# Engine order of first operations on fetched data, and a new order of value products, in a hybrid attention layer

## The chip, the core and the metric

The kernel runs on one core of a Trainium2 chip. The core has a matrix engine (TensorE, PE in the profile), three engines for elementwise work (VectorE or DVE, ScalarE or ACT, GpSimd or POOL), and a queue engine (SyncE or SP) that issues transfers. Each engine works through its own list of instructions strictly in order, and waits on semaphores for the others. Sixteen DMA engines carry the transfers of all queues. The metric is the device time of one execution in microseconds; lower is better.

## The reference

One decoder layer with two groups of heads, over 512 tokens of width 2048, in float32:

```
h = rms_norm(x, g_pre);  proj = h @ w_in
q_lat, kv_lat, k_rope, gate_mla, fq, fk, fv, f_logit, gate_fox = split(proj)
o_mla = softmax_causal(MLA scores of q_lat, kv_lat, k_rope) @ v  * silu(gate_mla)
c = cumsum(log_sigmoid(f_logit + b_forget))
o_fox = softmax_causal(fq·fk * scale + c_q - c_k) @ fv           * silu(gate_fox)
out = x + rms_norm(concat(o_mla, o_fox) @ w_out, g_post)
```

There are 8 MLA heads and 8 FoX heads of width 128. The change touches the first third of the work: the first projection, the gates, queries, keys and values of the FoX heads, and the FoX scores.

## The kernel before

**Arithmetic.** A float32 operand is kept as two parts, hi (rounded to the matrix engine's format by an ACT copy) and lo (the rest, by a DVE subtraction); a product is three matrix passes, hi·hi, hi·lo and lo·hi (mm3, L142 to L144). So each weight chunk that is fetched (tile raw) goes through one ACT cast (whi, L269) and one DVE subtraction (wlo, L272) before PE can use it. Casts and subtractions run two chunks ahead of PE, loads four chunks ahead (chunk).

**Products.** Some columns of the input projection (the FoX values, called v, and others) are computed by Winograd's variant of Strassen's scheme: seven products p1, p2, p4, q6, g3, g5, g7 of half-size blocks, of x blocks or sums of them, with weight blocks or sums of them. The sums of x blocks are made on DVE, written to memory by POOL (away_steps) and fetched back (fetch) into slots, where part_fetched splits them into hi and lo. Sums of weight blocks are of two kinds. Some are joined on chip: a chunk brings a second tile, and join adds it (L259). The others are made in memory by **background steps**: add_step copies one block (on SP's queue, L305) and a POOL transfer adds the other to it (L302). A small write called mark (L307), from a weight tile that is cast just then, paces them. set_pace(n) says that one step is made every n tiles; paced counts one tile per k step in projections and products, whether it belongs to the steps' own work or not. The first projection isn't counted. There are 36 steps, and state["pace"] is 6 at the start. load asserts that a step is far enough on when its sum is loaded.

**Order of the first third.** proj_first (L576), a projection for the forget logits and part of the latents, in 16 k steps; its engines' order is fixed by hand (manual_schedule). Then fox_g(0) (gate projection), product p1, fox_g(1), p2, fox_g(2), g5, fox_q(0), g3, p4, q6, fox_k(0), g7. A gate, q or k projection has 16 k steps, a product 8. scaled and scaled_copy combine the products' results into the blocks c11, c12, c21, c22 of the values; v_out writes them to memory, load_v fetches them by pairs of heads, split_v splits them. Then four rounds of two FoX heads follow: queries, scores, keys, values, each pumped as small steps from the list todo between the matmuls of the next projection. enqueue_scores and enqueue_values fill that list; drain runs what is left of it.

**Who sets an engine's order.** Outside the hand-ordered part a scheduler takes, at compile time, any instruction whose inputs it models as ready, so that one may go ahead of earlier ones of its engine's program. keep_in_program_order takes an instruction out of that: it stays behind those that come ahead of it in the program on its engine. Before the change only the join's addition (L259) and, in a late stage, the weight cast are pinned so.

**Other work on fetched data.** rotary_tables fetches the positions (pos, L803) and makes sine and cosine in 20 steps on DVE and ACT, the first being the cast of L811. forget_keys negates a fetched row c per head (nk, L789) and adds the mask.

**Memory.** Most tiles of 4 KB per partition come from 28 common slots (slot). The values' blocks and the table's tiles come from a pool of their own (vr, v_room), which is closed after g7, so that the heads' tiles (pp) take its place.

Of the kernel before, what the change touches and what calls it, by code (L numbers as in the profile page):

```python
# [65 lines left out]
def tile_hybrid_layer(  # L66
# [61 lines left out]
            act.mul(to, src[:, :P], scale)  # L128
        return to

    def split_into(hi, lo, src, scale=None):
        if scale is None:
            act.copy(hi, src)
            dve.tensor_tensor(out=lo, in0=src, in1=hi.bitcast(F32), op=ALU.subtract)
        else:
            act.mul(hi, src, scale)
            dve.scalar_tensor_tensor(  # L137
                out=lo, in0=src, scalar=scale, in1=hi.bitcast(F32), op0=ALU.mult, op1=ALU.subtract
            )
# [132 lines left out]
        dve.tensor_tensor(out=lo[:, :m], in0=raw[:, :m], in1=hi[:, :m].bitcast(F32), op=ALU.subtract)  # L272
        ready[i] = [t[:, :m].rearrange("p (k c) -> p k c", k=n) for t in (hi, lo)]

    state = {"loaded": 0, "divided": 0, "tiles": 0, "step": -1, "pace": 6}

    def prepare(i):
        while state["divided"] < min(len(chunks), i + 1):
# [80 lines left out]

    first = add_chunks(w_in, [(0, O_KR - L4, KL), (KL, O_F, NH)], NK, 2, KL + NH, single=2)  # L360
    fox = [{} for _ in range(4)]
    for n in ("g0", "p1", "g1", "p2", "g2", "s5", "q0", "s3", "p4", "s6", "k0", "s7",
              "q1", "k1", "q2", "k2", "q3", "k3", "g3"):
        name = {"p1": "p1", "p2": "p2", "p4": "p4", "s5": "g5", "s3": "g3", "s6": "q6", "s7": "g7"}.get(n)
        if name:
            add_products([(name, "v")], plain_in)
        else:
            at = {"q": O_FQ, "k": O_FK, "g": O_GF}[n[0]] + 256 * (3 - int(n[1]))
            fox[int(n[1])][n[0]] = add_chunks(w_in, [(0, at, 256)], NK, 4, 256)
# [416 lines left out]
    def forget_keys(both, h):  # L786

        nk, nkm = both[:, 0, :], both[:, 1, :]
        dve.tensor_scalar(out=nk, in0=nk, scalar1=-1.0, scalar2=None, op0=ALU.mult)  # L789
        for b in range(NT):  # L790
            c = slice(b * P, (b + 1) * P)
            dve.tensor_tensor(out=nkm[:, c], in0=nk[:, c], in1=mask, op=ALU.add)
        return nk, nkm, h
# [5 lines left out]
    def rotary_tables():  # L799
# [7 lines left out]
        def names():  # L807
            nonlocal n1, n2
            nn = vr.tile([P, 2, S], F32, tag="c", name="nn")
            n1, n2 = nn[:, 0, :], nn[:, 1, :]  # L810
            dve.tensor_copy(n1, pi)  # L811
            dve.tensor_scalar(out=r, in0=n1, scalar1=ifc[:, 0:1], scalar2=None, op0=ALU.mult)

        n1 = n2 = None
# [148 lines left out]

    def part_fetched(n, of, j):
        both = oper[n, of][j]
        split_into(both[:, 0], both[:, 1], both[:, 1].bitcast(F32))

    def divisions(n, of):
        return [lambda j=j: part_fetched(n, of, j) for j in range(2 if of == "o" else 4)]
# [106 lines left out]
            ] + [pp.tile([P, 256], F32, tag="v3", name=f"{name}3", bufs=2)]  # L1076
        return v_tiles[name]

    def values_into(tiles, cols, parts, scale=lambda t: None):
        for t in range(NT - 1):  # L1080
            hi, lo = tiles[t]
            split_into(hi[:, cols], lo[:, cols], parts[t], scale(t))
        if scale(NT - 1) is None:
            act.copy(tiles[NT - 1][:, cols], parts[NT - 1])
        else:
            act.mul(tiles[NT - 1][:, cols], parts[NT - 1], scale(NT - 1))

    def values_of(name):
        tiles = v_tiles.pop(name)
# [40 lines left out]
    def split_v(pair, both):  # L1130

        tiles = v_pair(f"fv{pair}")
        return lambda: values_into(tiles, slice(0, 256), [both[:, t, :] for t in range(NT)])

    gates, gate_slots = {}, {}

# [12 lines left out]
    def v_block(name):  # L1149
        return vr.tile([P, 2, S], F32, tag="c", name=name)  # L1150
# [7 lines left out]
    def two_of(make, name):  # L1158
        return [make(f"{name}{i}") for i in range(2)]
# [18 lines left out]
    todo.extend(fs[:13])  # L1178
    fox_g(0, [att_bank("fg00"), bank("pv", "fg01", 1)])
    drain()  # L1180
    rot = rotary_tables()
    rot.append(rotary_key)
    wait(1)
# [16 lines left out]
    todo.extend([*x_steps(2), *x_steps(3)])  # L1200
    fox_g(2, two_of(proj_bank, "fg2"))
    drain()
    set_pace(16)
    f3, f6, f7 = (fetches(n, "m") for n in ("g3", "q6", "g7"))
    d3, d6, d7 = (divisions(n, "m") for n in ("g3", "q6", "g7"))
    G = two_of(att_bank, "vg")
# [1 line left out]
    c22 = v_block("vc22")  # L1208
    scaled(c22, G, 2, pb, ALU.subtract, rcol)
    todo.extend([*f3, *rot[10:14], *d3, *rot[14:]])  # L1210
    q, wholes = fox_q(0)
    drain()
    todo.extend([*f6[:2], lambda: None, lambda: None, d6[0], f6[2], d6[1], f6[3]])
    product("g3", "v", operand("g3", "m"), G, False, True)
    drain()
    c12 = v_block("vc12")
    scaled(c12, G, 0, pa, ALU.subtract, rcol)
    wait(1)
    todo.append(d6[2])
    wait(2)  # L1220
    todo.append(d6[3])
    B = two_of(proj_bank, "vp4")
    product("p4", "v", x_block(1, 2), B, True, True)
    c21 = v_block("vc21")
    scaled(c21, B, 2, pb, col=rcol)
    drain()
    set_pace(10)
    C = two_of(proj_bank, "vc")
    product("q6", "v", operand("q6", "m"), C, True, True)
    scaled(c12, C, 0, c12, col=rcol)  # L1230
    v_out(c12, 0, 1)
# [538 lines left out]
```

## Time and profile before

| what | us |
|---|---|
| three runs, median | 936.87 |
| lowest and highest | 936.67, 938.46 |
| the profiled execution, own time | 936.87 |
| its span in the profile | 935.1 |
| PE at work | 895.9 |

A row of the timeline gives start, length, engine, source line, operation, output tile and input tiles, and in brackets how long the engine stood idle just before and what ended that. A row of the busy times by stage gives the window, its length, then for each engine the microseconds at work and the number of instructions, then the clock granted to PE (1.00 is full), the mean share of the 16 DMA engines in use, and GB/s. A row of the waits gives who waited for whom, the sum, the number of times, and the longest. PE's matmuls overlap, so starts, not lengths, show its rate.

### The profile page before, as it was taken

The page shows a single profiled execution, that of the slowest core. Times are in us where ns is not written, and L with a number is a line of the kernel's source. Part 1 is how long each engine was busy: PE and PEld are TensorE (multiplying, and loading weights), DVE is VectorE, ACT ScalarE, POOL GpSimd, SP SyncE. Part 2 cuts the span into 40 slices and gives each one's busy share as a digit, 9 for nine tenths or more (in the row PEclk, how much of TensorE's full clock was granted, in tenths as well). Part 3 has the DMA queues.
Part 4 walks back from the last instruction along what each step waited for, and adds up shares of the span by engine and source line. Part 5 has one row for each costly group of instructions (what it writes and reads, how often), then busy time and mean ns, then how long its engine had stood idle before and what let it go on. Part 6 is the DMA issues. An engine that isn't in the chain of part 4 may idle for free.

```text
span 935.1 us, 12821 instructions
## 1 busy us (share of the span) xinstructions
PE 895.9 (96%) x4594; PEld 761.3 (81%) x4594; DVE 679.5 (73%) x1120; ACT 453.6 (49%) x836; POOL 65.8 (7%) x86
## 2 busy tenths in 40 slices
PE   4999996999999999999999999999999999999997
PEld 4988884777887887888999899878888888888885
DVE  1979783486368573766759879877779896897875
ACT  3684331344334341433455545654556566655474
POOL 1000220001021100100000000000000000000021
PEclk8899998899999999999999999999999999999998
DMA  9468999668899988889689998578843234789878
GB/s 296 119 198 234 287 303 342 195 221 265 220 281 256 248 206 226 237 207 266 147 310 399 345 332 291 136 176 202 217 110 107 68 113 159 247 313 304 282 221 251
DMA packets 125515, 218.26 MB, mean 233 GB/s; under 512 B 16362, under 2 KB 53764, under 8 KB 124428
## 3 DMA queue, kind: packets, MB, share of 16 engines
q1 hardware_dynamic: 113340, 179.41, 59.2%
q0 software_dynamic: 11376, 37.75, 19.5%
q8 instruction: 36, 0.59, 0.3%
q10 hardware_dynamic: 736, 0.29, 0.1%
q14 instruction: 27, 0.22, 0.1%
HBM read 202.72 MB, written 65.03 MB: 286 GB/s over the span
## 4 chain that ended last, share of the span: by engine, by line
PE 80%; DMA 10%; DVE 5%; ACT 3%; issue 1%; SPq 1%; POOL 0%; ACTq 0%; DVEq 0%
PE fk L142 3%; PE fk L143 3%; PE fk L144 3%; PE fg L142 3%; PE fg L143 3%; PE fg L144 3%; PE in L576 3%; PE fq L142 2%; PE fq L143 2%; PE fq L144 2%; PE sm L619 2%; DVE wlo L272 2%; DMA second<-in_w_in_dram 2%; DMA raw<-in_w_in_dram 2%; PE oa L144 2%; PE oa L143 2%
## 5 line engine op out<-in xcount | busy, mean ns | idle before, releaser
L272 DVE TENSOR_TENSOR wlo<-raw,whi 128x1024 fp32r<-128x1024 f32 (+3 forms) x217 | 256.2, 1187 | 118.7 <-ACT whi L269 109.7
L269 ACT CAST whi<-raw 128x1024 fp32r<-128x1024 f32 (+3 forms) x217 | 220.8, 1023 | 240.5 <-PE fg L143 28.0
L142 PE MATMUL fk<-h,whi 128*128 128x512 f32 x128 | 53.9, 421 | 0.0
L143 PE MATMUL fk<-h,whi 128*128 128x512 f32 x128 | 51.2, 400 | 0.0
L144 PE MATMUL fk<-h,wlo 128*128 128x512 f32 x128 | 51.2, 400 | 0.0
L142 PE MATMUL fq<-h,whi 128*128 128x512 f32 x128 | 50.8, 397 | 0.0
L142 PE MATMUL fg<-h,whi 128*128 128x512 f32 x128 | 50.3, 393 | 0.0
L144 PE MATMUL fq<-h,wlo 128*128 128x512 f32 x128 | 50.0, 390 | 0.0
L143 PE MATMUL fq<-h,whi 128*128 128x512 f32 x128 | 49.9, 390 | 0.0
L144 PE MATMUL fg<-h,wlo 128*128 128x512 f32 x128 | 49.9, 390 | 0.0
L143 PE MATMUL fg<-h,whi 128*128 128x512 f32 x128 | 49.9, 389 | 0.0
L259 DVE TENSOR_TENSOR raw<-raw,second 128x1024 f32<-128x1024 f32 x32 | 39.0, 1218 | 10.7 <-DMA second<-in_w_in_dram 10.6
L576 PE MATMUL in<-whi,h 128*128 128x328 f32 x128 | 30.8, 329 | 12.5 <-DVE h L137 12.5
L641 ACT ACTIVATE pf<-sf,stf 128x128 f32<-128x128 f32 (+3 forms) x32 | 16.8, 525 | 33.9 <-DVE stf L634 33.9
L576 PEld LDWEIGHTS in<-whi,h 128*128 128x128 f32 x128 | 22.1, 195 | 12.7 <-DVE h L137 12.7
L144 PEld LDWEIGHTS fk<-h,wlo 128*128 128x128 f32 x128 | 24.8, 193 | 5.7
L142 PE MATMUL mq<-ln,whi 128*128 128x512 f32 x72 | 29.0, 402 | 0.0
L142 PEld LDWEIGHTS fk<-h,whi 128*128 128x128 f32 x128 | 24.7, 193 | 4.7 <-issue 0.2
L143 PEld LDWEIGHTS fk<-h,whi 128*128 128x128 f32 x128 | 25.0, 195 | 4.1
L144 PEld LDWEIGHTS fq<-h,wlo 128*128 128x128 f32 x128 | 24.0, 188 | 5.3
L144 PEld LDWEIGHTS fg<-h,wlo 128*128 128x128 f32 x128 | 24.0, 188 | 5.2
L143 PE MATMUL mq<-ln,whi 128*128 128x512 f32 x72 | 28.2, 392 | 0.0
(556 smaller groups left out, 2481.0 us busy)
## 6 DMA issues: line engine op xcount, KB each, us to landing
raw<-in_w_in_dram SPq DMA_DIRECT2D x96, 512.0 KB
raw<-in_w_out_dram SPq DMA_DIRECT2D x32, 512.0 KB
second<-in_w_in_dram SPq DMA_DIRECT2D x24, 512.0 KB
bmg<-awaymg SPq DMA_DIRECT2D x20, 256.0 KB
awaymg<-rmg POOLq DMA_DIRECT2D x8, 512.0 KB, 10.8
raw<-t6v SPq DMA_DIRECT2D x8, 512.0 KB
t7o<-in_w_out_dram SPq DMA_DIRECT2D x4, 1024.0 KB
t7o<-in_w_out_dram POOLq DMA_DIRECT2D x4, 1024.0 KB, 10.3
```

The lines of the kernel that those rows point to most:

```text
L142: pe.matmul(o, ah, bh, start=first, stop=False, **kw)
L143: pe.matmul(o, ah, bl, start=False, stop=False, **kw)
L144: pe.matmul(o, al, bh, start=False, stop=last, **kw)
L259: tc.keep_in_program_order(dve.tensor_tensor(out=raw, in0=raw, in1=second, op=ALU.add))
L269: cast = act.copy(hi[:, :m], raw[:, :m])
L272: dve.tensor_tensor(out=lo[:, :m], in0=raw[:, :m], in1=hi[:, :m].bitcast(F32), op=ALU.subtract)
L576: pe.matmul(banks[t][:, :n], a[k][:, tss[t]], b[:, j, :], start=k == 0 and m == 0, stop=k == NK - 1 and m == 2,)
L619: pe.matmul(s[:, :nn], a[:, qs], c[:, :nn], start=(i == 0), stop=(i == len(pairs) - 1))
L641: act.activation(p, s[:, :n], AF.Exp, bias=st[:, 0:1], scale=unit, accum_out=st[:, 1:2])
```

## The change

- in_order(...) pins instructions with keep_in_program_order. Pinned are: both halves of the split of a fetched operand (part_fetched), the split of fetched values (split_v, and the last plain copy in values_into), the negation in forget_keys (L789), and the cast of the positions (L811).
- fox_k(0) moves from between q6 and g7 to between g3 and q6, and p4 from ahead of q6 to behind it; the weights' list is ordered to match (k0 and p4 change places). The fetches and splits of q6's operand go from g3 and p4 into fox_k(0), those of g7's operand from fox_k(0) into p4 and g7.
- The pace is 4 up to the end of fox_g(0), then 20 up to g5's end, 8 from fox_q(0) to fox_k(0), 12 from q6 to g7 (before: 6 up to fox_g(2)'s end, 16 from g5 to p4, 10 from q6 to g7).
- The last sums c22 and c21 go to common slots (vo22, vo21) rather than over their first operand in the values' pool.

```diff
+    def in_order(*instructions):
+        for i in instructions:
+            tc.keep_in_program_order(i)
...
-    def split_into(hi, lo, src, scale=None):
+    def split_into(hi, lo, src, scale=None, pin=False):
         if scale is None:
-            act.copy(hi, src)
-            dve.tensor_tensor(out=lo, in0=src, in1=hi.bitcast(F32), op=ALU.subtract)
+            a = act.copy(hi, src)
+            b = dve.tensor_tensor(out=lo, in0=src, in1=hi.bitcast(F32), op=ALU.subtract)
+            if pin:
+                in_order(a, b)
...
-    state = {"loaded": 0, "divided": 0, "tiles": 0, "step": -1, "pace": 6}
+    state = {"loaded": 0, "divided": 0, "tiles": 0, "step": -1, "pace": 4}
...
-    for n in ("g0", "p1", "g1", "p2", "g2", "s5", "q0", "s3", "p4", "s6", "k0", "s7",
+    for n in ("g0", "p1", "g1", "p2", "g2", "s5", "q0", "s3", "k0", "s6", "p4", "s7",
...
-        dve.tensor_scalar(out=nk, in0=nk, scalar1=-1.0, scalar2=None, op0=ALU.mult)
+        in_order(dve.tensor_scalar(out=nk, in0=nk, scalar1=-1.0, scalar2=None, op0=ALU.mult))
...
-            dve.tensor_copy(n1, pi)
+            in_order(dve.tensor_copy(n1, pi))
...
-        split_into(both[:, 0], both[:, 1], both[:, 1].bitcast(F32))
+        split_into(both[:, 0], both[:, 1], both[:, 1].bitcast(F32), pin=True)
...
-        return lambda: values_into(tiles, slice(0, 256), [both[:, t, :] for t in range(NT)])
+        return lambda: values_into(tiles, slice(0, 256), [both[:, t, :] for t in range(NT)], True)
...
     fox_g(0, [att_bank("fg00"), bank("pv", "fg01", 1)])
     drain()
+    set_pace(20)
...
-    set_pace(16)
...
     todo.extend([*f3, *rot[10:14], *d3, *rot[14:]])
+    set_pace(8)
     q, wholes = fox_q(0)
     drain()
-    todo.extend([*f6[:2], lambda: None, lambda: None, d6[0], f6[2], d6[1], f6[3]])
     product("g3", "v", operand("g3", "m"), G, False, True)
-    drain()
     c12 = v_block("vc12")
     scaled(c12, G, 0, pa, ALU.subtract, rcol)
-    wait(1)
-    todo.append(d6[2])
-    wait(2)
-    todo.append(d6[3])
-    B = two_of(proj_bank, "vp4")
-    product("p4", "v", x_block(1, 2), B, True, True)
-    c21 = v_block("vc21")
-    scaled(c21, B, 2, pb, col=rcol)
+    todo.extend([*f6, *[lambda: None] * 3, *d6])
+    k = fox_k(0, wholes)
+    forget_cols()
     drain()
-    set_pace(10)
+    set_pace(12)
     C = two_of(proj_bank, "vc")
     product("q6", "v", operand("q6", "m"), C, True, True)
     scaled(c12, C, 0, c12, col=rcol)
     v_out(c12, 0, 1)
-    todo.extend([*f7, *[lambda: None] * 3, *d7])
-    k = fox_k(0, wholes)
-    forget_cols()
+    todo.extend([*f7, *d7[:2]])
+    B = two_of(proj_bank, "vp4")
+    product("p4", "v", x_block(1, 2), B, True, True)
     drain()
-    product("g7", "v", operand("g7", "m"), C, False, True)
-    scaled(c22, C, 2, c22, col=rcol)
+    c21 = v_block("vc21")
+    scaled(c21, B, 2, pb, col=rcol)
+    product("g7", "v", operand("g7", "m"), C, False, True, side=d7[2:])
+    c22, c22_sum = slot("vo22"), c22
+    scaled(c22, C, 2, c22_sum, col=rcol)
     v_out(c22, 1, 1)
-    scaled(c21, C, 2, c21, col=rneg)
+    c21, c21_sum = slot("vo21"), c21
+    scaled(c21, C, 2, c21_sum, col=rneg)
     v_out(c21, 1, 0)
```

More of the change, by code (lines that the diff above doesn't have):

```diff
@@ L1077, in v_pair, with values_into @@
         return v_tiles[name]
-    def values_into(tiles, cols, parts, scale=lambda t: None):
+    def values_into(tiles, cols, parts, pin=False):
         for t in range(NT - 1):
             hi, lo = tiles[t]
[L1082 to L1086, printed above, removed]
+            split_into(hi[:, cols], lo[:, cols], parts[t], pin=pin)
+        last = act.copy(tiles[NT - 1][:, cols], parts[NT - 1])
+        if pin:
+            in_order(last)
     def values_of(name):
```

## The prediction

> **What bounds the kernel now.** I read the page first, then the busy time by stage (cut where PE changes from one product to the next), then who made PE wait, then the timeline at each of those places.
>
> ```profile
> span 935.1 us, 12821 instructions
> PE 895.9 (96%) x4594; PEld 761.3 (81%) x4594; DVE 679.5 (73%) x1120; ACT 453.6 (49%) x836; POOL 65.8 (7%) x86
> ```
>
> PE works 895.9 of 935.1 us, so every microsecond that goes must be one in which PE stood still or ran slowly. The stages, with PE's clock:
>
> ```profile
> core 0: us, PE busy (x) PEld busy (x) DVE busy (x) ACT busy (x) POOL busy (x), PEclk, DMA share, GB/s
> 12.80:25.30 12.50, 0.04 (x2) 0.02 (x1) 1.65 (x4) 0.94 (x5) 0.00 (x0) 0.60 1.07 338
> 25.30:56.80 31.50, 31.50 (x213) 31.36 (x214) 29.11 (x50) 25.70 (x78) 0.00 (x0) 0.94 0.38 107
> 56.80:79.70 22.90, 22.90 (x104) 18.69 (x104) 17.92 (x33) 13.43 (x25) 4.00 (x4) 1.00 0.90 253
> 79.70:145.00 65.30, 65.30 (x290) 54.09 (x289) 51.04 (x66) 25.97 (x31) 11.64 (x15) 1.00 0.97 281
> 145.00:169.70 24.70, 15.41 (x49) 11.25 (x48) 12.56 (x15) 7.22 (x10) 1.43 (x2) 0.79 0.95 311
> 169.70:191.50 21.80, 21.80 (x97) 18.02 (x96) 6.35 (x7) 4.22 (x5) 1.19 (x1) 1.00 0.66 186
> 191.50:214.80 23.30, 21.37 (x91) 16.12 (x89) 21.88 (x28) 12.34 (x19) 0.66 (x1) 1.00 0.73 243
> 260.70:288.60 27.90, 26.20 (x120) 21.27 (x120) 18.41 (x43) 10.42 (x23) 5.00 (x6) 1.00 1.01 297
> 288.60:345.00 56.40, 56.40 (x263) 46.66 (x262) 39.05 (x89) 21.60 (x49) 9.10 (x10) 0.97 0.95 244
> 345.00:360.00 15.00, 12.70 (x55) 10.01 (x55) 8.02 (x20) 4.30 (x11) 0.61 (x2) 0.89 0.91 213
> 455.00:640.00 185.00, 183.20 (x1161) 164.63 (x1160) 147.15 (x192) 100.43 (x137) 4.67 (x8) 1.00 0.82 271
> ```
>
> From 360 us on the change brings only pins, of heads' and operands' splits, and PE stands little: 1.8 of 185 us from 455 to 640. Before that it is short in five places: the first projection (12.8 to 56.8), value product g5 (145.0 to 169.7), g3 with p4 (191.5 to 214.8), and two joints in the FoX heads (288, 355). What PE waited for in g5 (us in total, times, longest):
>
> ```profile
> PE vg L142 <- ACT whi L269: 8.1, 2, 4.8
> PE vg L143 <- DVE wlo L272: 1.2, 2, 0.8
> ```
>
> ACT and DVE are named, but here and at the other places the timeline shows them standing behind an instruction that waits for a transfer:
>
> ```profile
> 17.65 0.42 SPq L803 DMA_DIRECT2D pos<-in_positions_dram  x1
> 23.62 0.43 DVE L811 CAST nn<-pos 128x512 f32<-128x512 int32 x1 [13.93 <-DMA pos<-in_positions_dram]
> 25.28 1.46 PE L576 MATMUL in<-whi,h 128*128 128x328 f32 x4 [12.46 <-DVE h L137]
> 151.37 1.22 DVE L259 TENSOR_TENSOR raw<-raw,second 128x1024 f32<-128x1024 f32 x1 [9.53 <-DMA second<-in_w_in_dram]
> 153.86 0.50 PE L142 MATMUL vg<-whi,smg 128*128 128x512 f32 x1 [3.30 <-ACT whi L269]
> 162.02 1.25 ACT L133 CAST bmg<-bmg 128x512 fp32r<-128x512 f32 x2 [7.16 <-DMA bmg<-awaymg]
> 164.26 0.79 PE L142 MATMUL vg<-whi,smg 128*128 128x512 f32 x1 [4.76 <-ACT whi L269]
> 275.59 1.02 ACT L133 CAST fv3h<-fv 128x256 fp32r<-128x256 f32 x3 [5.92 <-DMA fv<-v_away]
> 355.33 0.43 DVE L789 TENSOR_SCALAR nk<-nk 128x512 f32<-128x512 f32 x1 [5.05 <-DMA nk<-c_dram]
> ```
>
> The cast of the positions (L811), which the program has only after the first gate projection, sits in the middle of the first projection: DVE idles 13.93 us and h, ready to be made, stands behind it. The same with bmg's cast before whi (162.02), fv3h (275.59) and nk (355.33). The one other case is the join at 151.37: its second summand itself is late.
>
> **The change part by part.**
>
> *Pins.* Each pinned first operation stays in its engine's place of the program, so the wait ahead of it moves to a place where the data has long landed.
>
> Start. Gone are 12.5 us of standing and the slow clock behind it: (1 - 0.94) x 31.5 = 1.9 us. Together **-14.4**. What is late next? PE then needs a k of the projection every 2.2 us or so; the last weight chunk issued ahead of x's last parts is on time:
>
> ```profile
> 9.90 7.29 DMA raw<-in_w_in_dram
> ```
>
> It lands at 17.2; it belongs to k = 8 and 9, six ks after k = 2, at which PE stopped at 12.8, so it is wanted near 26. All of x stands ahead of pos in SP's queue and is in by 23.6, while the last k runs near 42. So nothing takes the stall's place, I think; the loosest bound is that x's last parts cost some microseconds.
> The table work that DVE did between the h's (row below) has to be done elsewhere.
>
> ```profile
> L828 DVE SCALAR_TENSOR_TENSOR pos<-nn,pos x15: 677/685/693, 27.3 to 49.5; 128x512 f32<-128x512 f32 x15
> ```
>
> 15 x 0.685 = 10.3, and ten more of the table's steps, none longer: at most 17 us of DVE, now between p1 and q0. DVE has 65.3 - 51.0 = 14.3 us free from 79.7 to 145 and 21.8 - 6.4 = 15.4 in q0: room of 29.7 for 17. I take nothing; if the cover were gone it would be at most 17.
>
> g5. It lasts 24.7 us. The same number of matmuls in g3 runs from the one of these rows to the other:
>
> ```profile
> 191.52 0.39 PE L142 MATMUL vg<-whi,bmg 128*128 128x512 f32 x1
> 202.40 0.39 PE L142 MATMUL vp<-whi,h 128*128 128x512 f32 x1
> ```
>
> That is 10.9, so g5 loses 13.8: 9.3 of standing (8.1 + 1.2) and 4.5 of slow clock. The second stand (4.76) goes with bmg's pin. The first (3.30) goes only if the second summand lands earlier, which is the part of the paces.
>
> *Paces.* A background step copies 512 KB on SP's queue and adds 512 KB on POOL's.
>
> ```profile
> q1 hardware_dynamic: 113340, 179.41, 59.2%
> q0 software_dynamic: 11376, 37.75, 19.5%
> 137.72 15.05 DMA second<-in_w_in_dram
> ```
>
> q1: 0.592 x 935.1 / 179.41 x 0.524 MB = 1.6 us of all 16 engines for 512 KB; q0 likewise 2.5. A step is 4.1. Counting k tiles, before does 10 steps in g0, p1, g1, p2, g2 (64 tiles at 6); after does 4 in g0 (16 at 4) and 2 up to g5's end (56 at 20). Four steps fewer, 16.4 us of DMA taken from the 88 us up to 145, in which the share is 0.90 and 0.97; that leaves about 0.77. The 15.05 us of a late transfer should then be nearer the 7.29 of the raw above; it is needed about 10 us after issue (151.3 when it came, 3.3 + 0.8 too late). I take g5's whole **-13.8**.
> In q0, g3 and k0 there are 5 steps in place of about 2, at DMA shares of 0.66 and 0.73: 3 x 4.1 over 54 us adds 0.23, still under 1. q6's last operand is finished in the middle of k0, one product ahead of use. Nothing.
>
> *Order g5, q0, g3, k0, q6, p4, g7.* No matmul is added. In 191.5 to 214.8 DVE was busy 21.88 of 23.3: q's and rotary's ends, the bmq splits and four joins together. k0 (21.8 us, four chunks only) now takes the bmq splits. The 1.9 us (23.3 - 21.37) go: **-1.9**. But q6, p4 and g7 now follow one another: 32.6 us of PE (3 x 10.9). DVE's work for them:
>
> ```profile
> L272 DVE TENSOR_TENSOR wlo<-raw,whi 128x1024 fp32r<-128x1024 f32 x28 | 33.9, 1221 | 28.0 <-ACT whi L269 23.7 <-DMA t6l<-in_w_in_dram 4.2
> L259 DVE TENSOR_TENSOR raw<-raw,second 128x1024 f32<-128x1024 f32 x4 | 4.9, 1218 | 0.0
> L1116 DVE SCALAR_TENSOR_TENSOR vc<-vc,rcol,vc 128x512 f32<-128x512 f32 x4 | 2.8, 742 | 0.0
> L134 DVE TENSOR_TENSOR bmg<-bmg 128x512 fp32r<-128x512 f32 x4 | 2.7, 686 | 4.1 <-ACT bmg L133 4.1
> L792 DVE TENSOR_TENSOR nk<-nk,mask 128x128 f32<-128x128 f32 x8 | 1.8, 286 | 0.1
> L134 DVE TENSOR_TENSOR fv2l<-fv,fv2h 128x256 fp32r<-128x256 f32 x3 | 1.3, 420 | 0.0
> ```
>
> 12 wlo and 4 joins at 1.22 are 19.5; four operands and the four steps of k's end at 0.69, 5.5; four scalings of two at 0.74, 5.9: 30.9, or 0.95 of the time, as in the stretch that lost 1.9. I charge **+2**; bounds 0, and 10 if DVE's order is bad.
>
> *Heads.* fv's pins free ACT for 5.9 us at 270: gone are 1.7 of standing and (1 - 0.97) x 56.4 = 1.7 of slow clock, **-3.4**. nk's pin: 2.3 and (1 - 0.89) x 15 = 1.7, **-4.0**. In return fv3's and fv2's splits (3 of 0.42 each) come at q1's end, just ahead of the first probabilities, and nk's work (0.43 + 4 x 0.286 per head) ahead of the first scores: 2.5 and 3.1 us of DVE at joints. I charge **+1.5**; bounds 0 and 5.6.
> The clock terms here rest on the rows: 2.30 us of standing were followed by 0.89. The Trainium skill, "TensorE: Matmul & The Clock Gate", Part 1, has the clock fall to half after an idle window of about 3.4 us; by that rule neither short stand would cost clock, and the sum would be 3.4 us smaller. The trace shows otherwise, and I go by the trace.
>
> *Common places.* vo22 and vo21 are written in the 28 slots, where g7's operands come free as g7 ends; the scaling instructions are the same. It lets the heads' tiles start without the stores of c22 and c21. Nothing measurable: 0, bounds -1 and +3 (a slot that comes late).
>
> Also, 2 steps fewer are done by g7's end (13 against 15): later steps come 2 x 4.9 tiles later, in stages with PE at full. Nothing. The pins of the later operands' splits (part_fetched, from 455 us on) can give back at most the 1.8 us there, and cost as much if a split now comes late: 0.
>
> **Sum.** -14.4 - 13.8 - 1.9 - 3.4 - 4.0 = -37.5; +2 + 1.5 = +3.5; and I set aside 3 us for waits that a new order brings, somewhere within the bounds above. -31.0. The profiled execution took 936.87 us (span 935.1, 1.8 around it), which is also the median: 936.9 - 31.0 = **905.9**.
>
> **Rivals.**
> *The second summand is still late.* If it stands behind SP's own transfers rather than POOL's, one copy fewer in its stretch is worth 1.6 of 15.05: the first stand, 3.3 + 0.8, and half of the 4.5 of slow clock stay: 905.9 + 6.3 = 912.2. For it: SP sends the copies and the loads down one queue. Against: the share was 0.97 with POOL's adds in it. The Trainium skill, "DMA: Bandwidth & Descriptors", Queues, rings and completion order, says that an engine takes the queues in turn, packet by packet; by that POOL's work slows SP's by no more than half, and this rival gains.
> *DVE becomes the bound from q6 to g7.* Up to 10 in place of 2: 913.9. For it: 0.95. Against: joins run one chunk ahead.
> *x is what comes next at the start.* If x's last parts hold PE, some 10 of 14.4 come back: 915.9. Against: the landings above.
> *The pin does not hold nn.* Then 14.4 stay: 920.3. Against: join's pinned addition at 151.37 did stand in its place for 9.53 us, ahead of later work.
> *SP becomes the bound* (the slower side). A step's mark blocks SP until its chunk is cast:
>
> ```profile
> SPq L307 <- ACT whi L269: 71.9, 24, 5.4
> SPq L305 <- DMA t6o<-whi: 10.3, 3, 7.1
> ```
>
> 3.0 us on average, and up to 7.1 more for the copy behind it. In g0 a step comes every four tiles of 21.8 / 16 = 1.36 us, 5.4 us; from a hold of 5.4 on, loads fall behind. With 9 steps in g0 and q0 to k0 at 3.0 + 7.1 less hidden 5.4, 4.7 each, that is 42 us: 905.9 + 42 = 948, slower. Against: a step each six tiles, 8.2 us, cost PE nothing from 56.8 to 145.
>
> **How the numbers follow.** Forecast, 899 to 910: 0.62. Second late: 0.12. DVE: 0.09. x next: 0.05. Pin void: 0.04. SP bound: 0.05, in 0.02 of it with a hold that only takes back the gain. The remaining 0.03 is two of the small rivals at once, still faster. Range 898 to 917: below, all of the 37.5 and 1 us more; above, the first three rivals; some 0.15 stays out. A measurement tells 0.2%, about 2 us. Faster 0.95, same 0.02, slower 0.03.
>
> **What would show it.** No DVE row at L811 before 40 us, and the first gate matmul near 42 in place of 56.8: the pin is right. g5 at 11 us and no wait named whi in it: pins and paces right; one wait left with `second` behind it: the second rival. DVE over 0.95 with waits on wlo in p4 or g7: the third. No stands over 1 us at q1's or k2's ends. What would make me wrong most is a wait in a place where no such work stands now, since the order of each engine is made anew.

## The result, and the profile after

The changed kernel took 904.15 us in the median of four runs (903.03 to 905.69), the kernel before, run beside it, 936.77 (933.23 to 938.46): a ratio of 0.9658, 95% interval 0.9625 to 0.9691. The profiled execution took 903.03 us.

The head of the page, and its first part:

```profile
span 901.3 us, 12830 instructions
PE 885.5 (98%) x4594; PEld 755.4 (84%) x4594; DVE 678.0 (75%) x1120; ACT 454.2 (50%) x837; POOL 66.0 (7%) x86
```

The span is 33.8 us shorter. PE's own work is 10.4 shorter with the same 4594 matmuls; the other 23.4 are standing. Of the 10.4, 9.8 fall in the four stages whose clock was below 1.00 before (41.8 to 40.0 us up to the first gate matmul, 15.5 to 11.2 in g5, 55.6 to 53.8 from q1 to q2, 55.4 to 53.6 from q2 to q3). The busy times by stage, cut where PE changes from one stage to the next (first projection, fox_g(0), p1 to g2, g5, g3, then q6, p4 and g7, q1, k1 to q2, and the start of k2):

```profile
10.00:42.33 32.33, 32.33 (x232) 32.22 (x231) 17.81 (x28) 29.21 (x89) 0.00 (x0) 1.00 0.86 262
42.33:65.20 22.87, 22.87 (x105) 18.70 (x104) 17.81 (x33) 10.92 (x21) 4.04 (x4) 1.00 0.97 272
65.20:130.50 65.30, 65.30 (x290) 54.07 (x289) 63.76 (x92) 28.68 (x34) 9.13 (x13) 1.00 0.88 251
130.50:142.40 11.90, 11.15 (x49) 8.90 (x48) 9.88 (x11) 6.43 (x7) 0.00 (x0) 1.00 1.06 379
164.20:175.00 10.80, 10.80 (x49) 8.97 (x48) 10.12 (x14) 5.89 (x9) 0.00 (x0) 1.00 0.66 215
197.00:230.40 33.40, 33.29 (x149) 27.24 (x148) 26.35 (x30) 15.72 (x20) 2.41 (x3) 1.00 0.93 282
230.40:256.60 26.20, 25.75 (x120) 21.27 (x119) 17.39 (x43) 7.78 (x15) 4.96 (x6) 1.00 0.96 273
256.60:311.40 54.80, 53.68 (x258) 44.43 (x256) 38.56 (x89) 21.42 (x53) 10.80 (x11) 1.00 1.02 265
311.40:327.00 15.60, 15.60 (x79) 12.94 (x78) 9.20 (x17) 7.85 (x17) 2.00 (x2) 1.00 1.01 262
```

The clock column is 1.00 throughout; before it read 0.94, 0.79, 0.97 and 0.89 in four of these stages. The stretch from 65.2 to 130.5 now holds the table work that stood in the first projection: DVE is busy 63.76 of 65.3 us there, 0.98 of the time, and PE still never stops. The places where PE or ACT stood before, in the timeline (lines up to some 800 have moved by 7: the cast of the positions is L818, whi L276, wlo L279, the matmuls L149 to L151):

```profile
42.33 0.39 PE L149 MATMUL fg<-h,whi 128*128 128x512 f32 x1
75.45 0.42 DVE L818 CAST nn<-pos 128x512 f32<-128x512 int32 x1
130.41 1.22 DVE L266 TENSOR_TENSOR raw<-raw,second 128x1024 f32<-128x1024 f32 x1
132.86 1.28 ACT L701 ACT_TABLE_LOAD   x1
139.78 0.50 PE L150 MATMUL vg<-wlo,smg 128*128 128x512 f32 x1 [0.75 <-DVE wlo L279]
142.41 0.39 PE L149 MATMUL fq<-h,whi 128*128 128x512 f32 x1
251.98 1.05 ACT L276 CAST whi<-raw 128x1024 fp32r<-128x1024 f32 x1 [5.47 <-DMA t7l<-whi]
255.81 0.95 PE L626 MATMUL sf<-fk,fq 128*128 128x512 f32 x3 [0.45 <-ACT pf L648]
262.43 0.55 PE L657 MATMUL ptf<-ident,pf 128*128 128x128 f32 x3 [1.12 <-ACT pf L648]
```

The gates' first matmul is at 42.33 in place of 56.78, the cast of the positions runs at 75.45 without a wait, the join at 130.41 waits for no summand, and g5 takes 11.9 us with one stand of 0.75. One new wait has come: at 251.98 a weight's cast stands 5.47 us behind the mark of a background step.

Where it all went, from first matmul to first matmul of the stages in the two profiles (q0 to q3 are the FoX query projections; the last stage runs from the first of the four late head groups to the last product of the output, mix):

| stage | predicted | before | after | difference |
|---|---|---|---|---|
| up to the first gate matmul | -14.4 | 56.78 | 42.33 | -14.45 |
| g5 | -13.8 | 24.78 | 11.94 | -12.84 |
| q0 to q1 (order of products) | -1.9 + 2 | 91.00 | 87.96 | -3.04 |
| q1 to q2 (fv's pins) | -3.4 and part of +1.5 | 57.31 | 55.39 | -1.92 |
| q2 to q3 (nk's pin) | -4.0 and part of +1.5 | 57.71 | 53.58 | -4.13 |
| late heads and output | +3 set aside, no place named | 299.83 | 302.53 | +2.70 |

The stretches between these stages did not change by more than 0.12.

### The profile page after: what moved, and what is told of

Its sections match the earlier page's. It is cut to its first block, busy times and chain, and to the rows that moved or that the text cites. A ratio compares the mean times of both kernels' runs of the same rounds, so it can differ in the third digit from the quotient of the medians.

```text
span 901.3 us, 12830 instructions
## 1 busy us (share of the span) xinstructions
PE 885.5 (98%) x4594; PEld 755.4 (84%) x4594; DVE 678.0 (75%) x1120; ACT 454.2 (50%) x837; POOL 66.0 (7%) x86
## 4 chain that ended last, share of the span: by engine, by line
PE 74%; DVE 14%; DMA 6%; issue 3%; ACT 3%; SPq 0%; ACTq 0%; DVEq 0%
DVE wlo L279 4%; PE in L583 3%; PE fk L151 3%; PE fk L149 3%; PE fk L150 3%; PE fq L149 3%; PE fq L151 3%; PE fq L150 3%; PE sm L626 2%; PE mq L149 2%; PE mq L151 2%; PE mq L150 2%; ACT whi L276 1%; PE oa L149 1%; PE od L150 1%
## 5 line engine op out<-in xcount | busy, mean ns | idle before, releaser
L279 DVE TENSOR_TENSOR wlo<-raw,whi 128x1024 fp32r<-128x1024 f32 (+3 forms) x217 | 256.7, 1187 | 128.9 <-ACT whi L276 119.7
L276 ACT CAST whi<-raw 128x1024 fp32r<-128x1024 f32 (+3 forms) x217 | 221.2, 1023 | 256.8 <-issue 34.8
L149 PE MATMUL fk<-h,whi 128*128 128x512 f32 x128 | 52.4, 410 | 0.0
L149 PE MATMUL fq<-h,whi 128*128 128x512 f32 x128 | 50.8, 397 | 0.0
L149 PE MATMUL fg<-h,whi 128*128 128x512 f32 x128 | 50.3, 393 | 0.0
L151 PE MATMUL fk<-h,wlo 128*128 128x512 f32 x128 | 50.2, 392 | 0.0
L150 PE MATMUL fk<-h,whi 128*128 128x512 f32 x128 | 50.1, 391 | 0.0
L151 PE MATMUL fq<-h,wlo 128*128 128x512 f32 x128 | 50.0, 390 | 0.0
L151 PE MATMUL fg<-h,wlo 128*128 128x512 f32 x128 | 49.9, 390 | 0.0
L149 PE MATMUL mq<-ln,whi 128*128 128x512 f32 x72 | 28.8, 400 | 0.0
L151 PEld LDWEIGHTS fk<-h,wlo 128*128 128x128 f32 x128 | 24.0, 188 | 5.3
L151 PEld LDWEIGHTS fq<-h,wlo 128*128 128x128 f32 x128 | 24.0, 188 | 5.3
L151 PEld LDWEIGHTS fg<-h,wlo 128*128 128x128 f32 x128 | 24.0, 188 | 5.1
L151 PE MATMUL mq<-ln,wlo 128*128 128x512 f32 x72 | 28.2, 391 | 0.0
L150 PEld LDWEIGHTS fg<-h,whi 128*128 128x128 f32 x128 | 24.1, 188 | 4.7
L149 PEld LDWEIGHTS fg<-h,whi 128*128 128x128 f32 x128 | 24.0, 188 | 4.7
```

The costliest lines, as they stand in the source:

```text
L149: pe.matmul(o, ah, bh, start=first, stop=False, **kw)
L150: pe.matmul(o, ah, bl, start=False, stop=False, **kw)
L151: pe.matmul(o, al, bh, start=False, stop=last, **kw)
L276: cast = act.copy(hi[:, :m], raw[:, :m])
```

## The experiments

The theory: each pin takes a waiting instruction out of the way of work that was ready, the paces bring the second summand in time, and the amounts are those of the stages above. Rivals per run are in the expectations. All kernels are variants of the changed kernel unless said otherwise; the stages, in us, from the same first matmuls. A kernel with one run was measured once, and the kernel before, run beside each batch, has medians from 935.8 to 939.0, so the stages tell more than the times:

| kernel | time (runs) | first gate | g5 | q0 to q1 | q1 to q2 | q2 to q3 | late |
|---|---|---|---|---|---|---|---|
| before | 936.77 (4) | 56.78 | 24.78 | 91.00 | 57.31 | 57.71 | 299.83 |
| changed | 904.15 (4) | 42.33 | 11.94 | 87.96 | 55.39 | 53.58 | 302.53 |
| changed, once more | 902.40 (4) | 41.75 | 11.82 | 87.96 | 55.26 | 53.62 | 301.89 |
| all pins, old order and paces | 910.65 (4) | 42.14 | 19.48 | 89.56 | 53.47 | 53.58 | 302.67 |
| old paces | 908.76 (4) | 42.48 | 19.23 | 88.01 | 53.53 | 53.58 | 302.14 |
| no nn pin | 916.60 (1) | 57.69 | 10.88 | 87.95 | 56.14 | 53.58 | 301.03 |
| no operand pins | 906.42 (1) | 43.91 | 14.84 | 88.81 | 55.38 | 53.58 | 300.34 |
| no nk pin | 903.87 (1) | 42.77 | 11.76 | 88.20 | 55.92 | 53.58 | 302.32 |
| no value pin | 908.89 (1) | 42.39 | 11.77 | 87.94 | 60.96 | 53.58 | 302.93 |
| pins but nk's, old order and paces | 909.29 (1) | 42.44 | 19.26 | 89.68 | 53.45 | 53.58 | 301.55 |
| output operands not pinned | 901.47 (5) | 43.58 | 11.86 | 87.98 | 55.47 | 53.58 | 300.97 |
| second value load behind q1 | 901.94 (4) | 43.78 | 11.76 | 87.96 | 54.18 | 54.37 | 301.42 |
| both | 900.82 (5) | 42.59 | 11.80 | 87.97 | 53.66 | 54.37 | 301.20 |
| both, sines pinned | 900.39 (5) | 42.27 | 11.76 | 88.34 | 53.87 | 54.37 | 300.48 |

**Pins alone, and old paces.** The first takes the kernel before and adds every pin; the second takes the changed kernel, order and all, and puts the old paces back.

```diff
-    state = {..., "pace": 4}
+    state = {..., "pace": 6}
...
-    set_pace(20)
...
+    set_pace(16)
...
-    set_pace(8)
...
-    set_pace(12)
+    set_pace(10)
```

> The kernel before with all four kinds of pins and nothing else (old order, old paces, old places). If the gain is the pins': the start's 14.4 us go, of g5's loss the second stand with its share of slow clock (about 7), nk's 4.1 and the joint at q1 (about 2): near 909, with one wait of PE in g5 that has the late second summand behind it. If the paces and the order carry as much as the pins: 915 or more, because the background steps now have 14 us less to hide in before g5, and the first stand grows by some of that.

> The changed kernel with the paces of before (6 up to the third gate, 16 from g5, 10 from q6). If the late second summand in g5 was a matter of the background steps' load on the DMA engines: the first stand comes back, 4 to 6.5 us, so 908 to 910.5, and a join on DVE waits some 10 us for its second summand. If the pins alone cured g5: 904, g5 near 12 us.

Ratios to before: 0.9704 (0.9667 to 0.974) and 0.9693 (0.9645 to 0.9741). The start is all the pins'. g5 falls from 24.78 to 19.48 by pins and to 11.94 only with the new paces: 5.3 and 7.5. What is left at the old paces, in the timeline of the second kernel:

```profile
137.89 1.23 DVE L266 TENSOR_TENSOR raw<-raw,second 128x1024 f32<-128x1024 f32 x1 [7.22 <-DMA second<-in_w_in_dram]
140.38 0.80 PE L149 MATMUL vg<-whi,smg 128*128 128x512 f32 x1 [4.12 <-ACT whi L276]
141.64 0.80 PE L150 MATMUL vg<-wlo,smg 128*128 128x512 f32 x1 [0.46 <-DVE wlo L279]
```

PE names ACT, and one row above DVE's join is seen waiting 7.22 us for the second summand, as in the kernel before. So a pin cannot help this stand (the join is pinned already), only an earlier landing can.

How the paces make it land earlier is seen on SP. First SP's wait in the kernel with old paces (115 to 140) and its timeline, then the timeline of the changed kernel:

```profile
SPq L312 <- DMA t6l<-whi: 7.3, 1, 7.3
```

```profile
127.55 0.56 SPq L312 DMA_DIRECT2D t6l<-in_w_in_dram  x1
128.86 0.46 SPq L247 DMA_DIRECT2D second<-in_w_in_dram  x1
```

```profile
120.50 0.37 SPq L247 DMA_DIRECT2D second<-in_w_in_dram  x1
```

With old paces SP stands 7.3 us at the copy of a background step, which waits for that step's mark, and issues the second summand only behind it, at 128.86; its join starts 9.0 us later (137.89). In the changed kernel no step is issued between 112.19 and 141.35, the summand is issued at 120.50, as soon as the join ahead of it is done, and it has landed when its join comes up 9.9 us later (130.41). With the same 9.0 us an issue at 120.6, when the join ahead of it was done, would have been in time for 130.67, from where DVE waited; so the late issue alone explains this stand. In the kernel before two things add up: the summand was issued at 136.25, behind two such copies, and joined 15.1 us later; with pins alone it was issued at 123.38 and joined 14.3 us later. Why it takes longer there no run shows. (Which issue belongs to which join follows from their order; there are two places for second summands.) The DMA engines as a whole got little freer from the first gate matmul to g5, first the kernel before, then the changed one:

```profile
56.80:145.00 88.20, 88.20 (x392) 72.78 (x392) 68.96 (x98) 39.40 (x55) 15.64 (x19) 1.00 0.96 274
42.33:130.50 88.17, 88.17 (x393) 72.77 (x392) 81.57 (x124) 39.60 (x55) 13.17 (x17) 1.00 0.91 256
```

The share is 0.96 in the kernel before and 0.91 in the changed one, with ten marks of steps in the one stretch and five in the other.

The order of products is the difference of the two kernels in q0 to q1: 89.56 against 88.01, -1.55; the pins alone bring -1.44 there. And one thing goes the other way: from q1 to q2 both kernels with old paces take 53.5, the changed kernel 55.39. The new paces cost 1.9 there.

**Without nn's pin.**

```diff
-            in_order(dve.tensor_copy(n1, pi))
+            dve.tensor_copy(n1, pi)
```

> The changed kernel without the pin on the positions' cast. By the theory that this one cast held the first projection: the first gate matmul at 56 to 57 us in place of 42.3, and 918 to 919 in all. By the rival that the earlier start is partly lost again to waits further on: below 914.

```profile
25.49 1.46 PE L583 MATMUL in<-whi,h 128*128 128x328 f32 x4 [11.21 <-DVE h L144]
```

The stand is back, and with it 15.4 us ahead of the gates; the time is 916.60, about 2 less than expected. Of the 15.4, 1.1 come back in g5: with the table work back in the first projection it takes 10.88 us, the bare length of its matmuls. Another 1.5 come back in the late stage, and 0.75 are lost from q1 to q2, in this one run.

**Without the operands' pins.**

```diff
-        split_into(both[:, 0], both[:, 1], both[:, 1].bitcast(F32), pin=True)
+        split_into(both[:, 0], both[:, 1], both[:, 1].bitcast(F32))
```

> The changed kernel without the pins on the fetched operands' splits. By the theory that bmg's cast ahead of whi made g5's second stand: g5 goes from 11.9 us to 16 or more. By the rival that with fewer background steps the fetch is on time wherever the cast stands: g5 stays under 13. If these pins also cause the 2.7 us that the changed kernel loses again after the FoX heads (MLA heads and output product), those are gone here, else they stay.

```profile
139.40 1.27 ACT L138 CAST bmg<-bmg 128x512 fp32r<-128x512 f32 x2 [2.64 <-DMA bmg<-awaymg]
141.66 0.50 PE L149 MATMUL vg<-whi,smg 128*128 128x512 f32 x1 [1.26 <-ACT whi L276]
142.92 0.50 PE L150 MATMUL vg<-wlo,smg 128*128 128x512 f32 x1 [0.76 <-DVE wlo L279]
```

g5 takes 14.84: between the two expectations. bmg's cast stands ahead of whi again, but 2.64 us in place of 7.16, which fits data that lands earlier at the new paces. So pins and paces don't simply add in g5: either takes part of what the other would.

**Without nk's pin, in the changed kernel and in the old order.**

```diff
-        in_order(dve.tensor_scalar(out=nk, in0=nk, scalar1=-1.0, ...))
+        dve.tensor_scalar(out=nk, in0=nk, scalar1=-1.0, ...)
```

> The changed kernel without the pin of nk's first operation. My theory (nk's pin alone is worth the 4.1 us that the stage from q2 to k2 became shorter): DVE stands at nk's negation for some 5 us near 350, PE stands about 2 us there and runs slowly behind it, the stretch from q2's first matmul to q3's takes about 57.7 us (before 57.71) in place of 53.58, and the time is about 908. Rival (the shorter stage comes from background steps that now fall elsewhere, not from the pin): 53.6 us for the stretch and about 904.

> The kernel before with all pins but nk's (its old order and paces; with nk's pin too it took 910.65). Theory A (with the old order and paces nk's pin is what makes the stretch from q2 to q3 53.6 us long in place of 57.7, and the new paces bring the same by moving a step away from nk's load): a stand of DVE of some 5 us at nk and a stretch of about 57.7, 914 to 915. Theory B (the other pins already move the load or the split so that nk's pin is worth nothing): 53.6, 910 to 911.

The stretch that was 4.1 us shorter stays so in both: 53.58. In the timeline of the second, old order and old paces, DVE does stand at nk:

```profile
324.00 1.15 DVE L139 TENSOR_TENSOR plf<-ptf,phf 128x512 fp32r<-128x512 f32 x2
325.07 0.42 DVE L796 TENSOR_SCALAR nk<-nk 128x512 f32<-128x512 f32 x1
328.98 0.43 DVE L796 TENSOR_SCALAR nk<-nk 128x512 f32<-128x512 f32 x1 [3.49 <-DMA nk<-c_dram]
```

And its busy times in the whole stretch:

```profile
293.00:347.00 54.00, 54.00 (x262) 44.99 (x261) 35.32 (x77) 20.67 (x46) 6.12 (x7) 1.00 0.93 241
```

It stands 3.49 us, and PE is at work in all of the 54 us. Before it stood 5.05 at the same place and PE lost 2.30 and a slow clock. The difference is what was queued behind it. Before, in the timeline:

```profile
355.68 0.55 DVE L134 TENSOR_TENSOR plf<-ptf,phf 128x384 fp32r<-128x384 f32 x1
356.28 0.44 PE L143 MATMUL pvf<-plf,fv2h 128*128 128x384 f32 x1 [2.30 <-DVE plf L134]
```

The second of the probabilities' splits (plf, 384 wide) had been left behind the negation of nk; here both (x2 at 324.00) are made ahead of it. Ahead of them in this order stand the splits of the next values (fv1), which the values' pins put there. In the changed kernel without nk's pin the waits are 1.61 and 0.24 and PE doesn't notice those either. So nk's pin buys nothing in either kernel, where the values' pin stands beside it. The stretch is 53.58 also in the kernel without the values' pin (below), and there nk's pin does the work: both splits are made by 323, and the negation comes behind them, without a wait:

```profile
348.14 0.42 DVE L796 TENSOR_SCALAR nk<-nk 128x512 f32<-128x512 f32 x1
```

So either pin is enough, as far as they are what does it; a kernel with neither, but with the rest of the change, wasn't tried.

**Without the values' pin.**

```diff
-        return lambda: values_into(..., True)
+        return lambda: values_into(...)
```

> The changed kernel without the pins of fv's splits (first values of each pair of heads). My theory: ACT stands at fv's first cast for several us in q1, the weight splits stand behind it, and the stretch from q1's first matmul to q2's takes 57 to 60 us (changed kernel 55.39, before 57.31); time 906 to 908. Rival (ACT stands there anyway, at a weight's cast held by a background step's mark, so the pin no longer buys anything): 55.4 us and about 904.

```profile
249.91 1.02 ACT L138 CAST fv3h<-fv 128x256 fp32r<-128x256 f32 x3 [8.84 <-DMA fv<-v_away]
253.07 0.49 PE L626 MATMUL sf<-fw 128*128 128x128 f32 x2 [3.05 <-ACT pf L648]
```

ACT stands 8.84 us at fv3's first cast and PE 3.05 and then runs slowly: q1 to q2 takes 60.96, so this pin is worth 5.6 us in the changed kernel. The rival, that the mark of a step would hold ACT anyway, falls.

**The value load behind q1.** The new wait on the mark has a chain behind it. SP's waits in the changed kernel from 225 to 262, and its timeline there:

```profile
SPq L1133 <- DMA v_away<-vo: 10.0, 2, 8.6
```

```profile
243.10 2.07 SPq L1133 DMA_DIRECT2D fv<-v_away  x2
246.00 0.36 SPq L314 DMA_DIRECT2D t7l<-whi  x1
246.41 0.26 SPq L314 DMA_DIRECT2D t6l<-whi  x1
246.78 0.73 SPq L314 DMA_DIRECT2D t7m<-whi  x1
```

SP holds the value loads for 8.6 us until the stores of the last blocks have landed, and the marks of three steps come out in one bunch behind it; a mark reads from a tile of whi, and the row at 251.98 shows ACT's next cast waiting for the mark t7l. PE's stands of 0.45 and 1.12 (255.81 and 262.43), 1.6 of the 1.9 us, wait for ACT's pf behind that cast. The bunch alone does not do it: with the old paces SP stands 7.1 us at the same loads and three marks come out between 251.66 and 252.69, and no cast on ACT waits for one. The edit moves the second pair's load:

```diff
-        vt = load_v(3 - p)
+        if p != 1:
+            vt = load_v(3 - p)
         if p:
             q, wholes = fox_q(p)
             drain()
+            if p == 1:
+                vt = load_v(3 - p)
+                wait(4)
```

> The changed kernel with the second pair's value load (fv2) issued behind q1's projection in place of ahead of it, so that the queue SP does not stand at it for 8.6 us (it waits for v_away's stores) with weight loads and background steps behind it. Theory (that stand bunches the marks of three steps, whi stands 5.47 us behind them, and the 1.9 us by which the stretch from q1 to q2 is longer than with the old paces come from it): the stretch takes 53.5 us in place of 55.39 and the time is about 902.3. Rival 1 (the number of steps in q1 does it, not the stand): 55.4 and 904.2. Rival 2 (the load now comes late and its pinned split holds ACT at k1's start): over 55.4, 905 to 908.

```profile
SPq L1133 <- DMA v_away<-vo: 9.4, 1, 9.4
```

```profile
252.10 1.05 ACT L276 CAST whi<-raw 128x1024 fp32r<-128x1024 f32 x1 [4.32 <-DMA t7l<-whi]
```

Again SP's waits (231 to 260) and the timeline. The edit doesn't do what it was to do: the first pair's load stands at the same place for 9.4 us, and ACT still waits 4.32. Two marks are bunched in place of three, the stage takes 54.18 in place of 55.39, and 0.8 comes back from q2 to q3. With the next edit added it takes 53.66, and PE's two stands are gone although ACT still waits 4.04. That is in line with the chain, and does not prove it: what exactly makes up the 1.9 us stays open, though it is the new paces that bring them.

**The output product's operands, both edits, and the changed kernel again.**

```diff
-        split_into(..., both[:, 1].bitcast(F32), pin=True)
+        split_into(..., both[:, 1].bitcast(F32), pin=of == "m")
```

> The changed kernel with the operand splits pinned only for the value products (those tagged m), not for the output product's (tagged o). Theory (the 0.8 us that the output product lost from its first matmul to the end, 168.85 against 168.03 before, come from these pins): 168.0 us for that stretch or less, and about 903.2; if the MLA stages gain as they did without any operand pin, 902. Rival (run-to-run differences of these stages): 168.9 and 904.2.

> The changed kernel with two edits: the output product's operand splits not pinned, and the second pair's value load issued behind q1's projection. If what each gave alone adds up (MLA heads 1.1 to 1.4 us, q1 and k1 1.2 us, of which 0.8 came back in q2 and k2): first gate matmul to mix about 848 us in place of 850.2, and about 901. If both only moved the same late steps to a better place: about 902, no better than either alone.

> The changed kernel once more, on the chip and against the runs of before that the two versions of it have: 903 to 905.5, and again 850.2 us from the first gate matmul to mix. If the stages behind 590 us differ by more than 0.5 us from the first profile, then differences of 1 us between versions there say nothing.

The ratios to before are 0.9635 (0.9611 to 0.966), 0.9642 (0.9617 to 0.9667) for the value load alone, 0.9624 (0.9602 to 0.9646) for both, and 0.9638 (0.9618 to 0.9658) for the changed kernel itself. The intervals overlap. The same kernel differs between its two profiles by 1.0 us from the first late head group to the output's first matmul (133.68 and 132.69), and by 0.35 the other way from there to mix; without these pins it is 132.25. So the 0.1 to 0.5 us less in the output product show nothing. The changed kernel itself came out a little under what was expected of it, 902.40 and 849.3 us from the first gate matmul to mix.

One stand does show. The first matmul of the output product, in the timeline of the changed kernel and of the one without these pins:

```profile
723.66 0.51 PE L149 MATMUL oa<-whi,boa 128*128 128x512 f32 x1 [0.59 <-ACT mw L126]
```

```profile
723.44 0.47 PE L149 MATMUL oa<-whi,boa 128*128 128x512 f32 x1
```

With the pins ACT makes a cast of another operand (soa, 721.37) and a weight's cast (721.90) ahead of two small copies that PE waits for (mw, 723.32); without them the copies come first (721.74 and 722.16). The pinned casts themselves (boa) are done ten microseconds earlier, so the pins act through the order that the scheduler makes around them. PE's stand of 0.6 us is in each of the nine profiles above whose late stage has these pins, and in none of the four that leave them out (no operand pins, output operands not pinned, both, both with sines). The nine take 301.0 to 302.9 us there, the four 300.3 to 301.2, before 299.83. So 0.6 of the 2.7 us lost late are these pins' doing; the rest comes and goes between profiles, such as a stand of 1.34 at 626.98 that is 0.33 in the second profile of the same kernel.

Both edits together are at best 1.6 us ahead, by medians, and not shown to be.

**The sines pinned.** To take the table load out of the gates' way:

```diff
-            dve.tensor_scalar(out=r, in0=r, scalar1=lim, scalar2=-lim, ...)
+            in_order(dve.tensor_scalar(out=r, in0=r, scalar1=lim, scalar2=-lim, ...))
```

> The kernel with the two edits, and the first operation of the sines pinned too, so that sines and table load run in q0 and not ahead of g5's joins. Theory (the 1.06 us by which g5 is longer than its 10.88 come from the table load of 1.28 us that the gates need behind the sines, and from the joins behind the gates): g5 10.9 to 11.2 us, and 0.7 to 1 us less than the same kernel without this pin, about 900. Rival 1 (DVE, busy 0.98 up to there, is what is late): 11.9, no change. Rival 2 (the sines are late for the rotary steps of k in q0): g5 short, but q0 and g3 longer by 1 to 3, 901 to 903.

```profile
127.33 0.72 ACT L853 ACTIVATE sinT<-pos,ifc 128x512 f32<-128x512 f32 x1 [4.60 <-DVE pos L851]
132.62 1.28 ACT L701 ACT_TABLE_LOAD   x1
```

The sines stay at 127.33 (127.67 without the pin) and the table load ahead of the gates stays too, so g5 is unchanged at 11.76 and neither the theory nor its first rival was tested: the edit moved neither of the two. Its time, 900.39 (0.9619, 0.9592 to 0.9645), is that of the kernel with both edits.

## Why the prediction was right, and where it was not

905.9 us was said, 904.15 came. The steps:

- **The start: right, in cause and size.** -14.4 predicted, -14.45 measured; without the pin 15.4 are back. No load took the stall's place. The table work was said to be covered, and is, by DVE at 0.98 of its time with PE at full; its price is not quite nothing, though: the 1.06 us by which g5 is longer than 10.88 go when the table work is back at the start.
- **g5: right in cause, 1.0 too much.** -13.8 against -12.84. The split of the two stands (pin for bmg's, paces for the second summand's) is what the runs show, with 5.3 and 7.5. The rival "second summand still late" fell: in the changed kernel no join of g5 waits. But the step that gave this was wrong, and its result came in part by luck: the DMA share was to fall from 0.95 to 0.77 and so shorten the transfer; it fell from 0.96 to 0.91, and the summand is in time because SP no longer stands at steps' copies ahead of its issue, and because it lands within 9.9 us where it took up to 15.1. What the rival had for it, that copies and loads go down one queue, was part of how the summand came late; with fewer copies in the queue it is issued in time. The 15.05 us were misread too: that row runs from an issue at 137.72, itself 7.24 us long, to a cast at 152.76, behind the join of 151.37, and is no length of a transfer. The 1.06 that stay have the joins standing behind the gates' work and a table load of 1.28 (132.86) in the timeline; that this is the cause was argued from the order of the rows, and the run meant to show it moved nothing.
- **The order of products: the term that was mis-sized.** -1.9 and a charge of +2 were put down; -3.04 came. The gain was read as the time in which PE wasn't busy from 191.5 to 214.8, 1.9. By the starts of their first matmuls p4 and q6 together took 25.7 us before (202.40 to 228.10), where two products of 10.9 take 21.8: 3.9 more, so busy time alone missed half. By the stages of the runs, the pins bring 1.44 of it and the order 1.55. The charge never came: DVE is busy 26.35 of 33.4 us from q6 to g7, 0.79, not 0.95. The step counted 30.9 us as instructions times mean duration, eight scalings where five run there, and took no account of overlap: of DVE's groups in that stretch the counts times mean durations add up to 28.9, while the time at work is 26.35. A DVE instruction's row can be longer than the distance to the start of the next (1.23 us for a wlo at 197.86, the next at 199.01). The rival "DVE becomes the bound" fell with it.
- **fv's pins: right, and then half taken back.** -3.4 predicted; with old paces they and their fellows bring 57.31 to 53.5, -3.8. With the new paces only -1.92 is seen. That the steps done less by g7's end "come later, nothing" was the wrong step: the new paces cost 1.9 there. That the steps' marks come out late behind the value loads that hold SP fits this, and is not proven.
- **nk's pin: right amount, and more than one pin gives it.** -4.0 predicted, -4.13 came in that stretch, and none of it is lost when this pin alone is left out. The prediction did not see that the loss hangs on one split of the probabilities queued behind the wait, so that whatever puts this split ahead will do; the values' pins do so by their order, and without them nk's pin does.
- **The clock terms: right.** PE's busy time fell by 9.8 us in the four stages with a slow clock, and the prediction's clock terms add up to 9.8 (1.9 + 4.5 + 1.7 + 1.7). The Trainium skill, "TensorE: Matmul & The Clock Gate", Part 1, with its idle window of about 3.4 us, would have left out 3.4 us of the sum, at 909.3; the trace spoke against it and the runs bear the trace out (below).
- **What was set aside: +3 said, +2.7 came**, or 2.1 by the second profile, in the late heads and the output. That the two agree is luck: the 3 were for waits within the bounds of the terms before, and for the pins of the later operands' splits the prediction put 0. Of the 2.7, 0.6 is the stand that these pins bring at the output's first matmul; the rest isn't settled, and the same kernel differs by 0.64 between profiles.
- **What else was forecast.** The rival that makes the kernel slower, SP as the bound, did not come. "No stands over 1 us at q1's or k2's ends" holds, but one of 1.12 has come 6 us behind q1's end. The common places for c22 and c21 weren't tested by themselves; their 0 rests on the sum.

Of the profiled span 33.8 us went where 31.0 were forecast: 3.1 more in the order and 0.3 less given back late, against 1.0 less in g5, and small differences in the rest. So the closeness of the total is in part that of terms that missed both ways.

## What to carry to other kernels

Where an engine waits for a transfer, look at what is queued behind the waiting instruction and who needs it when: here 3.49 us of standing cost PE nothing and 5.05 us cost it some 4, by the place of one instruction. An instruction that is the first to touch fetched data, and that a scheduler may move ahead, is worth a pin where the data is wanted late and the engine has other work that is wanted earlier. But a pin also changes the order that is made of the other instructions, which cost 0.6 us at the output product. The pin cannot help where the data itself lands late: there look first at when the transfer is issued, and at what holds the queue ahead of it (7.3 us here). A pacing that thins traffic early moves it, so look again where it comes later: here it cost 1.9 us from q1 to q2.

## What the hardware showed

**How short a stand slows PE.** In the busy times by stage, the clock just behind a stand: first the kernel before (after a stand of 2.30), then the kernel without operand pins (after 1.26 and 0.76 close together), then the kernel without the values' pin (3.05), then a stand of the changed kernel and the clock behind it:

```profile
356.30:361.00 4.70, 4.70 (x15) 3.76 (x16) 3.01 (x10) 0.27 (x1) 0.85 (x1) 0.64 0.82 216
357.00:359.00 2.00, 2.00 (x6) 1.54 (x6) 2.00 (x7) 0.00 (x0) 0.00 (x0) 0.50 0.77 208
361.00:366.00 5.00, 5.00 (x28) 4.23 (x27) 2.61 (x3) 1.64 (x2) 0.00 (x0) 1.00 1.08 207
```

```profile
142.92:147.00 4.08, 4.08 (x12) 3.20 (x13) 4.08 (x5) 1.63 (x3) 0.00 (x0) 0.63 0.73 225
```

```profile
253.00:256.00 3.00, 2.93 (x9) 2.37 (x10) 2.92 (x8) 1.31 (x5) 0.00 (x0) 0.63 0.55 150
```

```profile
626.98 0.62 PE L626 MATMUL sm<-mk,mq 128*128 128x256 f32 x3 [1.34 <-ACT pm L648]
```

```profile
626.98:634.98 8.00, 8.00 (x42) 6.95 (x43) 6.44 (x19) 5.80 (x17) 0.00 (x0) 1.00 1.01 238
```

Single stands of 1.12 and 1.34 us left the clock at 1.00. After 2.30, after 1.26 and 0.76 within 2.5 us, and after 0.71 and 0.99 within 2.8 us (the kernel before, 285.92 and 287.70) it fell. The 0.63 and 0.64 are means of windows that begin or end at 1.00: in the middle it reads 0.50, and 128x512 matmuls start 0.43 us apart there and 0.23 behind it (from 360.50). The loss is (1 - 0.64) x 4.70 = 1.7 us, which at 0.50 is a slow stretch of 3.4 us. So the stand of 2.30 us cost 2.30 and another 1.7. Where the change lies, between a single stand of 1.34 and two that add up to 1.7, no run shows; 1.17 and 0.21 within a microsecond (213.87 and 214.82) left it at 1.00.

**DVE at 0.98.** From 65.2 to 130.5 us DVE was busy 63.76 of 65.3 us, with the joins and splits that PE needs among its work, and PE lost nothing there: a share of busy time close to one need not be a bound where the work that is wanted first comes first.
